# Forgetting-attention scores of a two-layer decoder trunk: float32r products over 128 stacked rows, with the forget gates' sums in a mask built on GpSimd

## The chip, the cores and the metric

The kernel runs on one core of one Trainium2 chip. The core has a matrix engine (TensorE, PE in the profile, with its weight loads shown apart as PEld), VectorE (DVE), ScalarE (ACT), GpSimd (POOL) and SyncE (SP), each working through its own instructions in order and waiting on the others through semaphores, and 16 DMA engines. The metric is device time of one execution in microseconds (us), the median over several runs; lower is better.

## The reference

Two layers of a decoder trunk over 256 tokens of width 1024: a half-step SwiGLU feed-forward, a mixer of three groups of attention heads, and another half-step feed-forward, each after an RMS norm. The change is in the third group of the mixer, C: eight heads of forgetting attention.

```python
SEQ = 256; DEPTH = 2; HEAD_DIM = 64; C_HEADS = 8; Q_BLOCK = 128

def forgetting_attention(q, k, v, log_f):
    scale = D ** -0.5
    c = jnp.cumsum(log_f, axis=1).transpose(0, 2, 1)
    def block(i):
        ...
        s = jnp.einsum('bqhd,bkhd->bhqk', qb, k).astype(jnp.float32) * scale
        s = s + cq[..., None] - c[:, :, None, :]
        s = jnp.where((key_pos[None, :] <= qpos[:, None])[None, None], s, -jnp.inf)
        p = jax.nn.softmax(s, axis=-1).astype(v.dtype)
        return jnp.einsum('bhqk,bkhd->bqhd', p, v)

cq = rms_norm(cq.reshape(B, S, C_HEADS, HEAD_DIM), c_q_norm)
ck = rms_norm(ck.reshape(B, S, C_HEADS, HEAD_DIM), c_k_norm)
log_f = jax.nn.log_sigmoid(cf.astype(jnp.float32) + forget_bias.astype(jnp.float32))
o_c = forgetting_attention(cq, ck, cv.reshape(B, S, C_HEADS, HEAD_DIM), log_f)
o_c = o_c * jax.nn.sigmoid(cg)
```

With h a head, q a query position and k a key position, a score is the scaled product plus c[q] - c[k], where c is the running sum of the log forget gates. Group A (four heads that share one key head, with a token indexer) and group B (four heads) have no such term.

## The kernel before

**Precision by splitting.** Weights arrive as float32 (tile `raw`, DMA on SyncE's queue, L91). For each unit of 128x1024, ScalarE casts the high part to float32r (`wh`, L117) and VectorE subtracts it to get the low part (`wl`, L121). This is called by `W.pump` some units ahead of their use. Products of a weight and an activation are then three float32r products instead of one in float32. Heads A and B use a cheaper form (`products`): a query of 64 columns is stacked with its own low part to 128 rows (`stack`, L718 and L719), a key is written twice to 128 rows, and the transposed key is split in a high and a low part (`keys_T`, L741 and L742). Two float32r products, high and low, then make one score. C's scores before the change are one float32 product over 66 rows: 64 of the head, one for c, one of ones. For that the tiles `cqa` and `cka` have 66 columns, the last two of which hold [c, 1] for queries and [1, -c] for keys.

**Order.** All instructions are put out in the order of the program (a manual schedule). In a mixer, the input projection runs in 32 steps (eight chunks of columns, four units each); work beside it is hung on a step number with `at_step`. `cumsum` at step 29 sums the gates by a product with a triangular matrix; `c_norm` at step 25 scales C's queries and keys on GpSimd. Then come the heads of A and C in one pipeline, together with the output projection: for i from 0 to 12, `scores(i)`, `flip(i-1)` (transposes the softmax weights), `exps(i)`, at i = 1, 3, 5, 7 `c_T` (transposes queries and keys of a pair of C heads), except at i = 3, 5, 7 and 12 a half of an output-projection block (`next(halves)`; after each second half a `W.pump`), at odd i `outT` (transposes finished outputs), and `values(i-1)`. Heads 0 to 3 are A's, 4 to 11 C's.

**Per head.** `scores` writes one PSUM bank; VectorE adds the mask, negates and takes the minimum along the row in one instruction for each query block (L1024, 128 and 256 columns); ScalarE takes the exponential (L1031, L1032); TensorE transposes (L1038); VectorE or ScalarE, by turns, copies to SBUF (L1040); TensorE multiplies with the values, which carry a column of ones for the row sum; VectorE takes the reciprocal (L1054) and scales (L1060 or L1063). PSUM tiles of the tag "gu" have four banks, the working tiles "tmp" nine buffers; both are handed round in the order in which the program asks, so that the next user waits for the last reader of the buffer's former content.

Of the kernel before, what the change touches and what calls it, by code (L numbers as in the profile page):

```python
# [10 lines left out]
F32 = mybir.dt.float32  # L11
# [130 lines left out]
def kernel(ctx: ExitStack, tc: tile.TileContext, x, ffn1_norm, ffn1_w_gate, ffn1_w_up, ffn1_w_down,  # L142
# [9 lines left out]
    sm = ctx.enter_context(tc.tile_pool(name="sm", bufs=4))  # L152
    at = ctx.enter_context(tc.tile_pool(name="at", bufs=1))
    pp = ctx.enter_context(tc.tile_pool(name="pp", bufs=2))
    psum = ctx.enter_context(tc.tile_pool(name="psum", bufs=4, space=PSUM))
    ctx.enter_context(tc.manual_schedule())

# [131 lines left out]
    cs = cst[:, 256:512].rearrange("p (t c) -> p t c", t=2)  # L289
    causal = cp.tile([P, 3 * P], F32, name="causal")  # L290
    identr = cp.tile([P, P], F32R, name="identr")
    cqa = [at.tile([P, 8, 66], F32, name=f"cqa{t}", tag=f"cqa{t}") for t in range(2)]
    cka = [at.tile([P, 8, 66], F32, name=f"cka{t}", tag=f"cka{t}") for t in range(2)]
    va = [at.tile([P, 13, 65], F32, name=f"va{t}", tag=f"va{t}") for t in range(2)]
    for t in range(2):
        G.memset(cqa[t][:, :, 65:66], 1.0)
        G.memset(cka[t][:, :, 64:65], 1.0)
        G.memset(va[t][:, :, 64:65], 1.0)


    def mm(o, l, r, start, stop):
        T.matmul(o, l, r, start=start, stop=stop, skip_group_check=True)  # L302
# [358 lines left out]
    def mixer(l, norm, nxt):  # L661
# [3 lines left out]
        def at_step(n, fn):  # L665
            side.append((n, next(count), fn))
# [7 lines left out]
        def heads(ap, n):  # L674
            return ap.rearrange("p (h d) -> p h d", h=n)
# [25 lines left out]
        def head_rs(ss, n, tag):  # L701
            return rsqrt(ss, ss, 1.0 / HD, n, tag)
# [6 lines left out]
        def evac(dst, ps, t, scale=None):  # L709
            A.activation(dst, ps, AF.Copy, scale=norm.r[:, t:t + 1])  # L710
# [33 lines left out]
        def products(o, q, k, start, stop):  # L744
            mm(o, q, k[0], start, False)
            mm(o, q, k[1], False, stop)
# [24 lines left out]
        def post_ib(ps):  # L771
# [98 lines left out]
            def cumsum():  # L870
                b = bank("acc")
                mm(b[:, 0:16], tri, lf.rearrange("p t h -> p (t h)"), True, False)
                mm(b[:, 8:16], ones, lf[:, 0], False, True)
                for t in range(2):
                    c = b[:, 8 * t:8 * t + 8]
                    A.copy(cqa[t][:, :, 64], c)
                    A.activation(cka[t][:, :, 65], c, AF.Copy, scale=-1.0)

            at_step(SUMS_STEP, cumsum)
        def post_a(ps):  # L880
            ss = sm.tile([P, 2, 5], F32, name="ssa", tag="ss")
            rot = [hp.tile([P, S], F32, name="aqr", tag="hl") for _ in range(2)]
            ak = [at.tile([P, 1, HD], F32, name=f"ak{t}", tag=f"ak{t}") for t in range(2)]
            akd = [at.tile([P, 2, HD], F32, name=f"akd{t}", tag=f"kd{t}") for t in range(2)]
            sq = []
            for t in range(2):
                evac(rot[t], ps[t][:, :256], t)
                evac(ak[t][:, 0], ps[t][:, 256:320], t)
                evac(va[t][:, 0, 0:64], ps[t][:, 320:384], t)
                sq.append(squares(ps[t][:, :320], t, 5))  # L890

            def a_rope(t):
                rope(heads(rot[t], 4), tab[:, 0, 0, t], tab[:, 0, 1, t])
                rope(ak[t], tab[:, 1, 0, t], tab[:, 1, 1, t])

            for t in range(2):
                at_step(A_ROPE + t, lambda t=t: a_rope(t))

            def a_norm():
                for t in range(2):  # L900
                    square_sums(ss[:, t], sq[t])
                rs = head_rs(ss.rearrange("p t h -> p (t h)"), 10, "a")
                for t in range(2):
                    scale_heads(akd[t], ak[t], rs[:, 5 * t + 4:5 * t + 5])
                st["ra"] = minus(rs, 10, "a")

            at_step(A_ROOT, a_norm)

            def a_split():
                st["aq"] = [stack(x) for x in rot]  # L910

            def a_turn():
                st["aqT"] = at.tile([P, 4, S], F32R, name="aqT", tag="qs")
                st["akT"] = at.tile([P, 2, 1, S], F32R, name="akT", tag="ikT")
                queries_T(st["aqT"], st["aq"])
                keys_T(st["akT"], [d.rearrange("p a b -> p (a b)")[:, None] for d in akd])

            at_step(A_TURN - 2, a_split)
            at_step(A_TURN, a_turn)
# [33 lines left out]
            run_heads([("B", h) for h in range(4)], qk_b, "acc", lambda i, fn: at_step(B_STEP + i, fn))  # L953

        c_ss = at.tile([P, 2, 2, 8], F32, name="c_ss", tag="c_ss")

        def c_sums(i, dst, ps, when):
            sq = []
            for t in range(2):
                evac(dst[t][:, :, 0:64], heads(ps[t], 8), t)  # L960
                sq.append(squares(ps[t], t, 8))

            def sums():
                for t in range(2):
                    square_sums(c_ss[:, i, t], sq[t])

            at_step(when, sums)

        def post_ck(ps):
            c_sums(0, cka, ps, 21)  # L970

        def post_cq(ps):
            c_sums(1, cqa, ps, 25)
            for t in range(2):
                q = cqa[t][:, :, 0:64]
                G.tensor_tensor(q, q, gc[:, None, :].to_broadcast([P, 8, HD]), op=ALU.mult)

            def c_norm():
                rs = head_rs(c_ss.rearrange("p i t h -> p (i t h)"), 32, "c")
                for t in range(2):  # L980
                    for i, d in enumerate((cka, cqa)):
                        x = d[t][:, :, 0:64]
                        scale_heads(x, x, rs[:, 16 * i + 8 * t:16 * i + 8 * t + 8])

            at_step(25, c_norm)

# [15 lines left out]
        def run_heads(hs, qk, tag, emit=None):  # L1002
            pj, pt, op = {}, {}, {}

            def scores(i):

                kind, h = hs[i]
                q, k = qk(kind, h)
                b = bank(tag)
                if kind == "C":  # L1010
                    mm(b[:, 0:P], q[:, 0:P], k[:, 0:P], True, True)
                    mm(b[:, P:3 * P], q[:, P:S], k[:, 0:S], False, True)
                else:
                    products(b[:, 0:P], q[:, 0:P], [c[:, 0:P] for c in k], True, True)
                    products(b[:, P:3 * P], q[:, P:S], [c[:, 0:S] for c in k], False, True)
                mask = st["amask"] if kind == "A" else causal
                s = tmp(3 * P)
                nm = sm.tile([P, 2], F32, name="nm", tag="nm")
                for t, c in enumerate((slice(0, P), slice(P, 3 * P))):
                    scale = -1.0  # L1020
                    if kind != "C":
                        col = (5 * t if kind == "A" else 4 * t) + h
                        scale = st["r" + kind.lower()][:, col:col + 1]
                    V.tensor_tensor_reduce(s[:, c], b[:, c], mask[:, c], scale, 3e38, op0=ALU.add, op1=ALU.min,  # L1024
                                           accum_out=nm[:, t:t + 1])
                pj[i] = (s, nm)
# [99 lines left out]

        halves = out_halves()

        c_both = xp.tile([P, 2, 8, S], F32, name="cT", tag="xhl")
        cT = [c_both[:, 0], c_both[:, 1]]  # L1130

        def c_T(hp_):
            for d, src in zip(cT, (cqa, cka)):
                b = bank("gu")
                for i in range(2):
                    for t in range(2):
                        T.transpose(b[:66, i * S + t * P:i * S + (t + 1) * P], src[t][:, 2 * hp_ + i, :], ident)  # L1137
                (A.copy if src is cqa else V.tensor_copy)(d[:66, 2 * hp_:2 * hp_ + 2],
                                                         b[:66].rearrange("p (a b) -> p a b", a=2))

        def qk_ac(kind, h):
            if kind == "A":
                return st["aqT"][:, h], [st["akT"][:, c, 0] for c in range(2)]
            return cT[0][:66, h], cT[1][:66, h]

        hs = [("A", h) for h in range(4)] + [("C", h) for h in range(8)]
        scores, exps, flip, values, outT = run_heads(hs, qk_ac, "gu")
        n = len(hs)
        next(halves)
        for i in range(n + 1):  # L1150
            if i < n:
                scores(i)
            if i > 0:
                flip(i - 1)
            if i < n:
                exps(i)
            if i in (1, 3, 5, 7):
                c_T(i // 2)
            if i not in (3, 5, 7, n):
                next(halves)  # L1160
            if 0 < i < n:
                if i > 2 and i % 2:
                    outT((i - 3) // 2)
                values(i - 1)
# [64 lines left out]
```

## Time and profile before

| | us |
|---|---|
| median of 3 runs | 1037.88 (1037.73 to 1037.98) |
| profiled execution | 1038.33 |
| span of its instructions | 1036.6 |
| granted TensorE clock | 1.00 |
| stage of heads A and C, layer 0 | about 291 to 327 |
| the same, layer 1 | about 804 to 843 |

The page of the profile gives for each engine its busy time and share of the span, the chain of waits that ended last, the costliest groups of instructions by line, and the DMA issues. The timeline of an engine lists start, busy time, engine, line, operation, output and inputs with partitions x elements, and in brackets the idle time before it and who ended it. Instructions of an engine overlap a little, so that the distance of two starts, and not the busy time, is what one costs; for TensorE the ends are modelled and the difference is large.

### The profile page before, as it was taken

How to read it: one execution, taken by the hardware profiler on the slowest of the kernel's cores; microseconds unless marked ns; L12 is line 12 of the kernel's file. 1: busy time of each engine (PE TensorE's matmuls, PEld its weight loads, DVE VectorE, ACT ScalarE, POOL GpSimd, SP SyncE). 2: the span in 40 equal slices, each digit the busy share in tenths (PEclk: the TensorE clock that was granted, in tenths of full speed). 3: DMA queues.
4: the chain of work that ended last, by engine and by line, in shares of the span. 5: the costliest groups of instructions: out<-in, count | busy, mean ns of one | idle time of the engine just before them, and what ended most of it. 6: DMA issues, size and time to landing. Idle time of an engine off the chain costs nothing.

```text
span 1036.6 us, 15084 instructions
## 1 busy us (share of the span) xinstructions
PE 1032.3 (100%) x5641; PEld 898.8 (87%) x5641; DVE 808.9 (78%) x1537; ACT 591.8 (57%) x1045; POOL 148.2 (14%) x177
## 2 busy tenths in 40 slices
PE   9999999999999999999999999999999999999998
PEld 8888888898888888888888888888988988888887
DVE  6978778789876877777788777787898768777776
ACT  6655555666854655555465555557676546555552
POOL 2003000167800000000000110002766000000000
PEclk9999999999999999999999999999999999999999
DMA  9674656555431364645645564664555224554631
GB/s 320 222 244 157 214 185 198 182 190 174 154 131 42 123 230 144 236 163 206 200 163 195 180 219 150 241 185 174 163 194 172 83 67 159 182 199 167 232 134 40
DMA packets 130808, 181.61 MB, mean 175 GB/s; under 512 B 7040, under 2 KB 104624, under 8 KB 130736
## 3 DMA queue, kind: packets, MB, share of 16 engines
q1 hardware_dynamic: 130704, 180.66, 51.5%
q8 instruction: 44, 0.72, 0.3%
q14 instruction: 28, 0.23, 0.1%
q10 hardware_dynamic: 32, 0.01, 0.0%
HBM read 179.60 MB, written 1.05 MB: 174 GB/s over the span
## 4 chain that ended last, share of the span: by engine, by line
PE 99%; DMA 1%; SPq 0%; DVE 0%; issue 0%
PE ps_gu L302 66%; PE ps_acc L302 30%; PE ps_acc L337 1%; PE ps_gu L1038 1%; PE ps_gu L1137 1%; DMA trunk<-in_x_dram 1%; PE ps_acc L739 0%; PE ps_acc L1038 0%; PE ps_gu L1071 0%; PE ps_acc L494 0%; SPq L91 0%; PE ps_acc L363 0%; PE ps_acc L1071 0%; SPq L190 0%; DVE trunk L376 0%
## 5 line engine op out<-in xcount | busy, mean ns | idle before, releaser
L121 DVE TENSOR_TENSOR wl<-raw,wh 128x1024 fp32r<-128x1024 f32 (+2 forms) x342 | 416.9, 1225 | 24.9 <-ACT wh L117 24.9
L117 ACT CAST wh<-raw 128x1024 fp32r<-128x1024 f32 (+2 forms) x341 | 343.0, 1036 | 5.7 <-PE ps_gu L302 4.9
L302 PE MATMUL ps_gu<-xhl,wh 128*128 128x512 f32 x1408 | 330.4, 390 | 0.0
L302 PEld LDWEIGHTS ps_gu<-xhl,wh 128*128 128x128 f32 x1408 | 262.7, 188 | 53.9 <-ACT wh L117 0.4
L302 PEld LDWEIGHTS ps_gu<-xhl,wl 128*128 128x128 f32 x1408 | 176.1, 191 | 4.2 <-issue 0.2
L302 PE MATMUL ps_gu<-xhl,wl 128*128 128x256 f32 x1408 | 179.1, 283 | 0.0
L302 PE MATMUL ps_gu<-wh,xhl 128*128 128x512 f32 (+2 forms) x512 | 157.2, 377 | 0.0
L441 DVE TENSOR_TENSOR tmp<-ps_gu,tmp 128x256 f32<-128x256 f32 x176 | 72.9, 422 | 107.7 <-ACT tmp L440 107.4
L302 PE MATMUL ps_acc<-wh,hh 128*128 128x512 f32 (+1 forms) x352 | 137.2, 390 | 0.0
L302 PE MATMUL ps_acc<-wl,hh 128*128 128x512 f32 (+1 forms) x352 | 137.0, 389 | 0.0
L302 PE MATMUL ps_acc<-wh,hl 128*128 128x512 f32 (+1 forms) x352 | 136.5, 388 | 0.0
L440 ACT COPY tmp<-ps_gu 128x256 f32<-128x256 f32 x176 | 63.5, 371 | 93.3 <-PE ps_gu L302 93.1
L302 PEld LDWEIGHTS ps_gu<-wh,xhl 128*128 128x128 f32 x512 | 94.8, 188 | 14.6
L455 ACT CAST hh<-tmp 128x256 fp32r<-128x256 f32 x80 | 32.6, 407 | 120.0 <-DVE tmp L452 120.0
L302 PE MATMUL ps_gu<-wl,xhl 128*128 128x512 f32 (+2 forms) x256 | 95.7, 374 | 0.0
L447 ACT ACTIVATE tmp<-tmp 128x256 f32<-128x256 f32 x88 | 36.9, 419 | 81.9 <-DVE tmp L445 81.6
L313 POOL TENSOR_TENSOR y_n<-msq,minus_half 128x2 f32<-128x2 f32 x6 | 6.8, 1141 | 529.7 <-DVE msq L312 529.7
L302 PEld LDWEIGHTS ps_acc<-wh,hl 128*128 128x128 f32 x352 | 66.1, 188 | 13.9
L302 PEld LDWEIGHTS ps_acc<-wh,hh 128*128 128x128 f32 x352 | 66.2, 188 | 12.6
L302 PEld LDWEIGHTS ps_acc<-wl,hh 128*128 128x128 f32 x352 | 66.3, 188 | 12.2
L302 PEld LDWEIGHTS ps_gu<-wl,xhl 128*128 128x128 f32 x256 | 48.2, 188 | 6.7
L326 ACT ACTIVATE xhl<-ps_acc,gT 128x256 fp32r<-128x256 f32 x48 | 19.1, 474 | 39.2 <-PE ps_acc L337 35.7
(221 smaller groups left out, 1010.8 us busy)
## 6 DMA issues: line engine op xcount, KB each, us to landing
raw<-in_ffn_w_down_dram SPq DMA_DIRECT2D x44, 1024.0 KB, 4.9
raw<-in_ffn_w_gate_dram SPq DMA_DIRECT2D x42, 1024.0 KB, 6.6
raw<-in_ffn_w_up_dram SPq DMA_DIRECT2D x42, 1024.0 KB, 7.5
raw<-in_w_in_dram SPq DMA_DIRECT2D x24, 1024.0 KB, 4.9
raw<-in_w_out_dram SPq DMA_DIRECT2D x8, 1024.0 KB, 4.9
raw<-in_w_in_dram SPq DMA_DIRECT2D x4, 768.0 KB, 4.9
raw<-in_w_in_dram SPq DMA_DIRECT2D x4, 656.0 KB, 4.0
raw<-in_ffn_w_gate_dram SPq DMA_DIRECT2D x3, 512.0 KB, 7.1
```

Of the source, the lines that this page charges most:

```text
L117: self.nc.scalar.copy(hv, src)
L121: (engine or self.nc.vector).tensor_tensor(lv, self.srcs[self.n_low], hv.bitcast(F32), op=ALU.subtract)
L302: T.matmul(o, l, r, start=start, stop=stop, skip_group_check=True)
L313: G.tensor_tensor(y, dst, minus_half[:, :n], op=ALU.pow)
L326: A.activation(self.h[:, m], src, AF.Copy, scale=gT[:, self.col + m:self.col + m + 1])
L337: T.transpose(ps[:, i, t * P:(t + 1) * P], trunk[:, t, (2 * mp + i) * P:(2 * mp + i + 1) * P], ident)
L440: A.copy(o, ps[:, 1])
L441: V.tensor_tensor(o, ps[:, 0], o, op=ALU.add)
L447: A.activation(th, t_, AF.Tanh, scale=0.5)
L455: (V.tensor_copy if late else A.copy)(hh, t_)
L1038: T.transpose(b[:, j * P:(j + 1) * P], pj[i][:, j * P:(j + 1) * P], ident)
L1137: T.transpose(b[:66, i * S + t * P:i * S + (t + 1) * P], src[t][:, 2 * hp_ + i, :], ident)
```

## The change

C's scores take the form that A's and B's have: two float32r products over 128 stacked rows. The term c[q] - c[k] is no longer in the product. Instead a mask of 128x384 for each head holds it together with the causal mask, and `scores` adds this mask where it added the causal one. The mask is built on GpSimd by four instructions a head (`decay`), two heads ahead. For it the sums are needed along a row, on every partition: they are transposed, negated and written to DRAM (`turn_sums`, step 30), and read back to all 128 partitions (`load_sums`, step 31, 1 MB in SBUF), both on ScalarE's DMA queue. Queries are still scaled in `c_norm`; keys are scaled on GpSimd as they are written twice, in `c_parts`, which stacks a pair's queries too. `c_T` keeps its places and writes a buffer for two pairs in turn.

```diff
@@ post_ib
                 b = bank("acc")
                 mm(b[:, 0:16], tri, lf.rearrange("p t h -> p (t h)"), True, False)
                 mm(b[:, 8:16], ones, lf[:, 0], False, True)
-                for t in range(2):
-                    c = b[:, 8 * t:8 * t + 8]
-                    A.copy(cqa[t][:, :, 64], c)
-                    A.activation(cka[t][:, :, 65], c, AF.Copy, scale=-1.0)
+                st["c"] = sm.tile([P, 2, 8], F32, name="c", tag="c", bufs=1)
+                A.copy(st["c"].rearrange("p t h -> p (t h)"), b[:, 0:16])
+
+            def turn_sums():
+                b = bank("acc")
+                for t in range(2):
+                    T.transpose(b[:8, t * P:(t + 1) * P], st["c"][:, t], ident)
+                n = tmp(S)[:8]
+                A.activation(n, b[:8, :S], AF.Copy, scale=-1.0)
+                st["row"] = dram.tile([8, S], F32, name="minus_c_row", tag="minus_c_row")
+                nc.scalar.dma_start(st["row"], n)
+
+            def load_sums():
+                d = st["row"]
+                st["minus_c"] = at.tile([P, 8, S], F32, name="minus_c", tag="kT")
+                nc.scalar.dma_start(st["minus_c"], bass.AP(tensor=d.tensor, offset=d.offset,
+                                                           ap=[[0, P], [S, 8], [1, S]]))
 
             at_step(SUMS_STEP, cumsum)
+            at_step(SUMS_STEP + 1, turn_sums)
+            at_step(SUMS_STEP + 2, load_sums)
@@ post_cq
             def c_norm():
                 rs = head_rs(c_ss.rearrange("p i t h -> p (i t h)"), 32, "c")
-                for t in range(2):
-                    for i, d in enumerate((cka, cqa)):
-                        x = d[t][:, :, 0:64]
-                        scale_heads(x, x, rs[:, 16 * i + 8 * t:16 * i + 8 * t + 8])
+                st["rk"] = rs[:, 0:16]
+                for t in range(2):
+                    scale_heads(cq[:, t], cq[:, t], rs[:, 16 + 8 * t:24 + 8 * t])
@@ scores
-                if kind == "C":
-                    mm(b[:, 0:P], q[:, 0:P], k[:, 0:P], True, True)
-                    mm(b[:, P:3 * P], q[:, P:S], k[:, 0:S], False, True)
-                else:
-                    products(b[:, 0:P], q[:, 0:P], [c[:, 0:P] for c in k], True, True)
-                    products(b[:, P:3 * P], q[:, P:S], [c[:, 0:S] for c in k], False, True)
-                mask = st["amask"] if kind == "A" else causal
+                products(b[:, 0:P], q[:, 0:P], [c[:, 0:P] for c in k], True, True)
+                products(b[:, P:3 * P], q[:, P:S], [c[:, 0:S] for c in k], False, True)
+                mask = decays.pop(h) if kind == "C" else st["amask"] if kind == "A" else causal
@@ mixer, heads A and C
-        def c_T(hp_):
-            for d, src in zip(cT, (cqa, cka)):
-                b = bank("gu")
-                for i in range(2):
-                    for t in range(2):
-                        T.transpose(b[:66, i * S + t * P:i * S + (t + 1) * P], src[t][:, 2 * hp_ + i, :], ident)
-                (A.copy if src is cqa else V.tensor_copy)(d[:66, 2 * hp_:2 * hp_ + 2],
-                                                         b[:66].rearrange("p (a b) -> p a b", a=2))
+        cT = xp.tile([P, 2, 4, 2, S], F32R, name="cT", tag="xhl")
+        beside = {}
+
+        def c_parts(j):
+            hs2 = slice(2 * j, 2 * j + 2)
+            q = tp.tile([P, 512], F32R, name="stacked", tag="tmp")
+            q4 = q.rearrange("p (t h s d) -> p t h s d", t=2, h=2, s=2)
+            A.copy(q4[:, :, :, 0], cq[:, :, hs2])
+            V.tensor_tensor(q4[:, :, :, 1], cq[:, :, hs2], q4[:, :, :, 0].bitcast(F32), op=ALU.subtract)
+            k = tmp(512)
+            k4 = k.rearrange("p (t h s d) -> p t h s d", t=2, h=2, s=2)
+            for t in range(2):
+                G.tensor_tensor(k4[:, t], ck[:, t, hs2, None, :].to_broadcast([P, 2, 2, HD]),
+                                st["rk"][:, 8 * t + 2 * j:8 * t + 2 * j + 2, None, None].to_broadcast([P, 2, 2, HD]),
+                                op=ALU.mult)
+            beside[j] = [x.rearrange("p (t h c) -> p t h c", t=2, h=2) for x in (q, k)]
+
+        def c_T(j):
+            q, k = beside.pop(j)
+            d = cT[:, j % 2]
+            bq, bk = bank("gu"), bank("gu")
+            for i in range(2):
+                for t in range(2):
+                    mm(bq[:, i * S + t * P:i * S + (t + 1) * P], q[:, t, i], identr, i + t == 0, True)
+            for i in range(2):
+                for t in range(2):
+                    T.transpose(bk[:, i * S + t * P:i * S + (t + 1) * P], k[:, t, i], ident)
+            bq, bk = (b.rearrange("p (h s) -> p h s", h=2) for b in (bq, bk))
+            A.copy(d[:, 0], bq)
+            A.copy(d[:, 1], bk)
+            V.tensor_tensor(d[:, 2], bk, d[:, 1].bitcast(F32), op=ALU.subtract)
+
+        def decay(h):
+            m = tmp(3 * P)
+            for t, (c, n) in enumerate(((slice(0, P), P), (slice(P, 3 * P), S))):
+                G.tensor_scalar(m[:, c], st["minus_c"][:, h, :n], st["c"][:, t, h:h + 1], None, op0=ALU.add)
+            for c in (slice(0, P), slice(2 * P, 3 * P)):
+                G.tensor_tensor(m[:, c], m[:, c], causal[:, c], op=ALU.add)
+            decays[h] = m
@@ the pipeline
+        c_parts(0)
         next(halves)
         for i in range(n + 1):
             ...
             if i in (1, 3, 5, 7):
                 c_T(i // 2)
+            if i in (2, 4, 6):
+                c_parts(i // 2)
+            if 2 <= i < 10:
+                decay(i - 2)
             if i not in (3, 5, 7, n):
                 next(halves)
```

More of the change, by code (lines that the diff above doesn't have):

```diff
@@ L154 @@
     pp = ctx.enter_context(tc.tile_pool(name="pp", bufs=2))
+    dram = ctx.enter_context(tc.tile_pool(name="dram", bufs=1, space=bass.MemoryType.DRAM))
     psum = ctx.enter_context(tc.tile_pool(name="psum", bufs=4, space=PSUM))
@@ L291 @@
     identr = cp.tile([P, P], F32R, name="identr")
-    cqa = [at.tile([P, 8, 66], F32, name=f"cqa{t}", tag=f"cqa{t}") for t in range(2)]
-    cka = [at.tile([P, 8, 66], F32, name=f"cka{t}", tag=f"cka{t}") for t in range(2)]
+    cq = at.tile([P, 2, 8, HD], F32, name="cq", tag="cq")
+    ck = at.tile([P, 2, 8, HD], F32, name="ck", tag="ck")
     va = [at.tile([P, 13, 65], F32, name=f"va{t}", tag=f"va{t}") for t in range(2)]
     for t in range(2):
-        G.memset(cqa[t][:, :, 65:66], 1.0)
-        G.memset(cka[t][:, :, 64:65], 1.0)
         G.memset(va[t][:, :, 64:65], 1.0)
@@ L955, in mixer @@
         c_ss = at.tile([P, 2, 2, 8], F32, name="c_ss", tag="c_ss")
+        decays = {}
         def c_sums(i, dst, ps, when):
@@ L959, in c_sums @@
             for t in range(2):
-                evac(dst[t][:, :, 0:64], heads(ps[t], 8), t)
+                evac(dst[:, t], heads(ps[t], 8), t)
                 sq.append(squares(ps[t], t, 8))
@@ L969, in post_ck @@
         def post_ck(ps):
-            c_sums(0, cka, ps, 21)
+            c_sums(0, ck, ps, 21)
         def post_cq(ps):
-            c_sums(1, cqa, ps, 25)
+            c_sums(1, cq, ps, 25)
             for t in range(2):
-                q = cqa[t][:, :, 0:64]
+                q = cq[:, t]
                 G.tensor_tensor(q, q, gc[:, None, :].to_broadcast([P, 8, HD]), op=ALU.mult)
@@ L1127, in mixer @@
         halves = out_halves()
-        c_both = xp.tile([P, 2, 8, S], F32, name="cT", tag="xhl")
-        cT = [c_both[:, 0], c_both[:, 1]]
-        def c_T(hp_):
-            for d, src in zip(cT, (cqa, cka)):
-                b = bank("gu")
-                for i in range(2):
-                    for t in range(2):
-                        T.transpose(b[:66, i * S + t * P:i * S + (t + 1) * P], src[t][:, 2 * hp_ + i, :], ident)
-                (A.copy if src is cqa else V.tensor_copy)(d[:66, 2 * hp_:2 * hp_ + 2],
-                                                         b[:66].rearrange("p (a b) -> p a b", a=2))
+        cT = xp.tile([P, 2, 4, 2, S], F32R, name="cT", tag="xhl")
@@ L1143, in qk_ac @@
                 return st["aqT"][:, h], [st["akT"][:, c, 0] for c in range(2)]
-            return cT[0][:66, h], cT[1][:66, h]
+            d = cT[:, h // 2 % 2]
+            return d[:, 0, h % 2], [d[:, 1, h % 2], d[:, 2, h % 2]]
         hs = [("A", h) for h in range(4)] + [("C", h) for h in range(8)]
```

## The prediction

> **What bounds the kernel now.** I read the page first, then the matmul engine's timeline through the stretch in which heads A and C are scored, then VectorE's and ScalarE's in the same stretch. Part 1 of the page and the chain of waits say that TensorE is the bound almost everywhere:
>
> ```profile
> PE 1032.3 (100%) x5641; PEld 898.8 (87%) x5641; DVE 808.9 (78%) x1537; ACT 591.8 (57%) x1045; POOL 148.2 (14%) x177
> ...
> PE 99%; DMA 1%; SPq 0%; DVE 0%; issue 0%
> ```
>
> So a cheaper product is worth its whole saving, but only as long as TensorE stays without gaps; and any wait that TensorE gains is a loss in full. The stage that changes runs from 291 to 327 us in layer 0 (and 804 to 843 in layer 1), in iterations i = 0 to 12: scores of head i, transposes ("flip") of head i-1, then in some iterations the transposes of a C pair (c_T) or half a block of the output projection, then the values of head i-1. TensorE's timeline (start, busy, engine, line, operation):
>
> ```profile
> 293.21 0.49 PE L1038 MATMUL ps_gu<-ident,p 128*128 128x128 f32 x3
> ...
> 296.93 0.49 PE L1038 MATMUL ps_gu<-ident,p 128*128 128x128 f32 x3
> ...
> 299.23 0.71 PE L302 MATMUL ps_gu<-akT,aqT 128*128 128x128 f32 x4
> 299.78 0.49 PE L1038 MATMUL ps_gu<-ident,p 128*128 128x128 f32 x3
> 300.11 0.60 PE L1137 MATMUL ps_gu<-ident,cqa 128*66 128x128 f32 x4
> 300.54 0.60 PE L1137 MATMUL ps_gu<-ident,cka 128*66 128x128 f32 x4
> 300.98 0.38 PE L1071 MATMUL ps_gu<-ident,o 128*128 128x128 f32 x2
> 301.27 0.88 PE L302 MATMUL ps_gu<-va,pT 128*128 128x65 f32 x6
> 301.99 0.87 PE L302 MATMUL ps_gu<-cT 66*128 66x128 f32 x4
> 302.70 0.49 PE L1038 MATMUL ps_gu<-ident,p 128*128 128x128 f32 x3
> ...
> 305.04 0.87 PE L302 MATMUL ps_gu<-cT 66*128 66x128 f32 x4
> ...
> 308.55 0.49 PE L1038 MATMUL ps_gu<-ident,p 128*128 128x128 f32 x3
> ...
> 314.40 0.49 PE L1038 MATMUL ps_gu<-ident,p 128*128 128x128 f32 x3
> ```
>
> The starts give the true prices, since busy times overlap. The flips of heads 1, 3, 5 and 7 (296.93, 302.70, 308.55, 314.40) are 5.77, 5.85 and 5.85 us apart, 17.47 together. These are my yardstick. VectorE and ScalarE over the first of these periods:
>
> ```profile
> 291.65 0.34 DVE L1024 CUSTOM_DVE_ANT_0 tmp<-ps_gu,amask,minus_a 128x128 f32<-128x128 f32 x1
> ...
> 297.81 1.22 DVE L121 TENSOR_TENSOR wl<-raw,wh 128x1024 fp32r<-128x1024 f32 x1
> 299.46 0.17 DVE L1054 RECIPROCAL ri<-ps_gu 128x2 f32<-128x2 f32 x1 [0.43 <-PE ps_gu L302]
> ...
> 299.98 0.35 DVE L1024 CUSTOM_DVE_ANT_0 tmp<-ps_gu,amask,minus_a 128x128 f32<-128x128 f32 x1
> ...
> 300.66 0.56 DVE L1040 COPY pT<-ps_gu 128x384 f32<-128x384 f32 x1
> 301.18 0.69 DVE L1138 COPY cT<-ps_gu 66x512 f32<-66x512 f32 x1
> ```
>
> ```profile
> 292.45 0.51 ACT L1032 ACTIVATE p<-tmp,nm 128x256 f32<-128x256 f32 x1
> ...
> 298.13 0.50 ACT L1032 ACTIVATE p<-tmp,nm 128x256 f32<-128x256 f32 x1
> ...
> 300.78 0.51 ACT L1032 ACTIVATE p<-tmp,nm 128x256 f32<-128x256 f32 x1
> ```
>
> The reader should see how little room there is in the iterations without a half of the output projection (3, 5, 7). VectorE's copy of the flipped weights ends at 301.22 and the values that read it start at 301.27. VectorE's whole slack in the first period is the 0.43 us before the reciprocal. An engine that is "78% busy" is here the second bound.
>
> **The change part by part: TensorE.** A C head's two fp32 products show as four records and cost 0.71 us (301.99 to 302.70); four float32r products of the same widths cost head A 0.55 (299.23 to 299.78). The saving is 0.16 us a head, 2.6 us for 16 heads. Transposing queries through the float32r identity costs (1.09-0.27)/7 = 0.117 each by the row below, against (0.60-0.27)/3 = 0.11 for today's, 0.27 being one record; four per pair make +0.03, eight pairs +0.24. The key transposes keep their number and streamed width: nothing. The sums' turn adds two transposes; such a pair costs 0.29 (outputs, 300.98 to 301.27), so 0.3 a layer, 0.6 in all. If nothing else moved, the sum were -2.6 + 0.24 + 0.6, about -1.8 us.
>
> ```profile
> 271.09 1.09 PE L302 MATMUL ps_acc<-identr,stacked 128*128 128x128 f32 x8
> ...
> 280.88 0.29 PE L302 MATMUL ps_acc<-lf,cst 128*128 128x16 f32 x2
> ```
>
> **The new chain in c_T.** Now one ScalarE copy and one VectorE copy run side by side, one for each PSUM bank. After the change ScalarE casts both banks in turn, and VectorE's subtraction of the keys waits for the second cast. The same pair of operations exists for B's keys, and the stacking for A's and B's queries (min/median/max in ns):
>
> ```profile
> L741 ACT CAST bkT<-ps_acc x4: 607/616/624, 243.2 to 756.8; 128x512 fp32r<-128x512 f32 x4
> L742 DVE TENSOR_TENSOR bkT<-ps_acc,bkT x4: 673/674/676, 246.9 to 760.6; 128x512 fp32r<-128x512 f32 x4
> ```
>
> ```profile
> L719 DVE TENSOR_TENSOR stacked<-bqr,stacked x4: 956/959/964, 233.9 to 747.8; 128x256 fp32r<-128x256 f32 x4
> L718 ACT CAST stacked<-aqr x4: 401/406/412, 262.6 to 776.0; 128x256 fp32r<-128x256 f32 x4
> L719 DVE TENSOR_TENSOR stacked<-aqr,stacked x4: 414/414/414, 263.6 to 777.0; 128x256 fp32r<-128x256 f32 x4
> ```
>
> The tag of these PSUM tiles has four banks, handed round in order. In iteration 5 they go to scores 5, flip 4, the two of c_T, outputs, values 4, scores 6, flip 5: so flip 5 takes the bank that the key subtraction still reads. Queued on VectorE behind that subtraction are the low parts of the outputs, the reciprocal, the output scaling and the next reduce.
>
> **The new chain in c_parts.** In iterations 2, 4 and 6 a 0.41 us copy stands on ScalarE behind the exponentials of head i, and VectorE's 0.41 us subtraction waits for it, with the weights' wl subtraction, the reciprocal and the next head's reduce queued behind.
>
> Worked for the first period, with the rows' durations and ScalarE's instructions overlapping by about 0.09 as they do now. Exponentials 2 end at 298.63; copy to 298.95; subtraction to 299.41, where VectorE before had worked on wl since 297.81; wl to 300.55; reciprocal, and 0.52 after its start the reduce of head 3 at 300.97 instead of 299.98. The flipped weights are copied at 302.20 (300.66 + 0.56, plus 0.99), values 2 start at 302.25 instead of 301.27. Exponentials 3 end 1.31 after the reduce begins (300.78 + 0.51 against 299.98), at 302.28; query cast to 302.8, key cast to 303.3; subtraction to 304.02; flip 3 at 304.07 instead of 302.70. **+1.37.**
>
> Second period (no wl, so the wait for the copy is covered by VectorE's idle time): flip 3 to scores 5 is still 2.34 us (302.70 to 305.04), scores 5 at 306.4, its reduce 0.13 late at 307.26, exponentials to 308.5, casts to 309.55, subtraction to 310.27, flip 5 at 310.32. That is 6.25 instead of 5.85. **+0.40**, with 0.16 saved on each of two scores and overrun by the casts.
>
> Third period (wl again): exponentials 6 end at 312.35, copy 312.67, subtraction 313.13, wl 314.27, reciprocal and scaling, reduce 7 at 314.80; flipped weights 315.90; exponentials 7 to 316.0, casts to 317.05, subtraction 317.77, flip 7 at 317.82: 7.50 instead of 5.85. **+1.65.** What is late next is every later instruction of TensorE, nothing absorbs it; from then on VectorE catches up, and heads 9 to 11 save 3 x 0.16 = 0.48.
>
> At the start the first subtraction of c_parts stands ahead of head 0's reduce (291.65): 0.41 later, against a slack of 0.25 between exponentials 0 (to 292.96) and flip 0 (293.21): +0.2. A layer: 1.37 + 0.40 + 1.65 - 0.48 + 0.2 + 0.3 = 3.4; two layers **+6.9 us**. Bounds: -1.8 in all if every cast and copy were covered, and upward the locks that follow.
>
> **GpSimd beside VectorE.** GpSimd is empty in this stage today. It gets, per head, 128 and 256 columns of tensor_scalar and twice 128 of tensor_tensor, and per pair twice 256 columns for the keys. Rows:
>
> ```profile
> 204.38 0.46 POOL L684 TENSOR_TENSOR swapped<-iqr,cst 128x128 f32<-128x128 f32 x1
> ...
> 217.52 0.75 POOL L686 TENSOR_TENSOR bqr<-bqr,swapped 128x256 f32<-128x256 f32 x1
> ...
> 277.19 1.05 POOL L691 TENSOR_TENSOR cqa<-cqa,y_c 128x512 f32<-128x512 f32 x1
> 278.19 2.03 POOL L691 TENSOR_TENSOR cka<-cka,y_c 128x512 f32<-128x512 f32 x1
> ```
>
> ```profile
> 277.25 4.05 DVE L121 TENSOR_TENSOR wl<-raw,wh 128x1024 fp32r<-128x1024 f32 x2
> ```
>
> No row has a tensor_scalar of that size with a column operand; I price it as the two-input rows (between nothing and twice that). A mask is 3 x 0.46 + 0.75 = 2.13 us, eight of them 17, the keys 8 x 0.75 = 6: 23 us a layer. The last rows show the two engines taking turns: two wl take 4.05 us beside GpSimd instead of 2 x 1.22, and GpSimd's 1.05 becomes 2.03; the stacking subtraction above takes 0.96 beside GpSimd and 0.41 without. So the subtraction may cost +0.5 and wl between +0.4 and +0.8, twice a layer on the path (periods one and three): between 0 and 2.6 a layer. I take 1.25, a half, since GpSimd waits for buffers part of the time: **+2.5 us.**
>
> [...]
>
> **The round trip through DRAM.** The sums' turn comes one step after the sums (280.88), the load one step later. An 8 KB transfer on ScalarE's queue landed in 2.6 us, 1 MB in 1 KB pieces in 6.6:
>
> ```profile
> raw<-in_ffn_w_gate_dram SPq DMA_DIRECT2D x42, 1024.0 KB, 6.6
> ...
> tmp<-in_ffn_norm_dram ACTq DMA_DIRECT2D x1, 8.0 KB, 2.6
> ```
>
> With steps of about 3 us the read is issued at 287 to 288 and lands at about 295; mask 0 is done by 297.5 and is read at 302. Cost nothing; the cover is 4 to 5 us. While ScalarE waits for the write, weight casts are queued behind, seven units ahead of their use. The small copies that go (four of the sums, GpSimd's two key scalings) lie beside other work.
>
> **Sum.** The profiled execution took 1038.33 us (span 1036.6), 0.45 over the median. 6.9 + 2.5 = 9.4: 1047.7 for such an execution, **1047.3 us** against the median.
>
> **Rivals.** (1) *The saving arrives.* If ScalarE and VectorE ran ahead enough, TensorE alone decides: 1037.88 - 1.8 = 1036.1, or 1035.3 without the turn's and cast's extras. For it: TensorE is the bound in 99% of the chain. Against: 0.05 us between copy and values. (2) *Half hidden.* The casts cost but c_parts' copy finds a gap: periods at +0.4 each, 1.2 - 0.48 + 0.5 = 1.2 a layer: 1040.3. (3) *GpSimd becomes the bound.* If its rows in company (2.03 for 1.05) hold for most of its instructions, 23 us become 37; begun at 295 they end at 332, where head 11 wants its mask near 323: +9 a layer, 1056. The same if the broadcast lands 9 us late. The point from which it decides is some 28 us of GpSimd work a layer. [...]
>
> **Chances.** Forecast 0.6, rival 1 0.12, rival 2 0.13, rival 3 0.15. The range takes in the forecast with its unknowns (6.9 less 4 to 6.9 plus 5.2, and somewhat over) and rival 2: 1039.5 to 1053. What a measurement of this kernel can tell from no change is 0.2%, 2.1 us; of rival 1 half lies beyond it. Faster 0.07, same 0.10, slower 0.83.
>
> **What would show it.** Right: flips of heads 3, 5 and 7 about 7, 6.3 and 7.5 to 8 us apart from the ones before, TensorE's idle time there put down to VectorE's key subtraction and to the flipped weights' copy, C scores at 0.55. Wrong: flips still under 5.85 apart (rival 1); the reduces of C waiting for GpSimd (rival 3); C scores not cheaper than 0.71, or VectorE reaching reduce 3 within 0.2 us of the scores' end.

## The result, and the profile after

| | before | after |
|---|---|---|
| median of 6 runs each, us | 1037.93 (1037.73 to 1038.24) | 1044.36 (1044.07 to 1044.82) |
| ratio | | 1.0062, 95% interval 1.0049 to 1.0075 |
| profiled execution, us (span) | 1038.33 (1036.6) | 1044.18 (1042.5) |

The change costs 6.4 us; 9.4 were forecast, and the time lies in the stated range. Parts 1 and 4 of the page after:

```profile
PE 1032.5 (99%) x5645; PEld 897.6 (86%) x5645; DVE 810.0 (78%) x1545; ACT 599.3 (57%) x1057; POOL 197.4 (19%) x249
...
PE 96%; ACT 2%; DVE 2%; issue 0%; POOL 0%; ACTq 0%; POOLq 0%
```

VectorE, at 0% before, and ScalarE, not among the entries before, now hold 4% of the chain. GpSimd's 49 us more hold none of it. TensorE's timeline in layer 0 (in brackets idle time and its releaser):

```profile
293.13 0.49 PE L1050 MATMUL ps_gu<-ident,p 128*128 128x128 f32 x3
...
296.83 0.49 PE L1050 MATMUL ps_gu<-ident,p 128*128 128x128 f32 x3
...
299.93 0.64 PE L301 MATMUL ps_gu<-identr,stacked 128*128 128x128 f32 x4
301.29 0.63 PE L1168 MATMUL ps_gu<-ident,tmp 128*128 128x128 f32 x4 [0.72 <-DVE o L1075]
301.87 0.44 PE L1083 MATMUL ps_gu<-ident,o 128*128 128x128 f32 x2
302.34 0.88 PE L301 MATMUL ps_gu<-va,pT 128*128 128x65 f32 x6
...
304.09 0.55 PE L1050 MATMUL ps_gu<-ident,p 128*128 128x128 f32 x3 [0.36 <-DVE cT L1172]
...
306.46 0.71 PE L301 MATMUL ps_gu<-cT 128*128 128x128 f32 x4
307.00 0.49 PE L1050 MATMUL ps_gu<-ident,p 128*128 128x128 f32 x3
...
310.24 0.55 PE L1050 MATMUL ps_gu<-ident,p 128*128 128x128 f32 x3 [0.36 <-DVE cT L1172]
...
314.88 0.63 PE L1168 MATMUL ps_gu<-ident,tmp 128*128 128x128 f32 x4 [0.84 <-DVE o L1072]
...
317.56 0.55 PE L1050 MATMUL ps_gu<-ident,p 128*128 128x128 f32 x3 [0.37 <-DVE cT L1172]
```

Flips 1, 3, 5 and 7 stand at 296.83, 304.09, 310.24 and 317.56: the periods are 7.26, 6.15 and 7.32 us, against 5.77, 5.85 and 5.85. That is +3.26 for the three. Heads 8 to 11 take back some: the flip of head 11 comes 2.66 us later than before in layer 0 (328.94 for 326.28), and layer 1 adds 2.74 between the flips of heads 0 and 11. Together 5.4 us of the span's 5.9. A quarter of a microsecond more is the turn of the sums in layer 1: from the gates' product to head 0's scores TensorE takes 10.26 us there, 10.01 before. The rest falls behind TensorE's last product. A product's cheapness is there: 0.54 us from the scores of head 5 (306.46) to the next flip, where 0.71 stood.

VectorE and ScalarE over the first period:

```profile
298.87 0.74 DVE L1150 TENSOR_TENSOR stacked<-cq,stacked 128x256 fp32r<-128x256 f32 x1 [1.07 <-ACT stacked L1149]
299.53 1.21 DVE L121 TENSOR_TENSOR wl<-raw,wh 128x1024 fp32r<-128x1024 f32 x1
...
300.85 0.29 DVE L1075 TENSOR_TENSOR o<-ps_gu,ri 128x128 f32<-128x128 f32 x1
301.06 0.34 DVE L1036 CUSTOM_DVE_ANT_0 tmp<-ps_gu,amask,minus_a 128x128 f32<-128x128 f32 x1
...
303.35 0.69 DVE L1172 TENSOR_TENSOR cT<-ps_gu,cT 128x512 fp32r<-128x512 f32 x1 [1.06 <-ACT cT L1171]
```

```profile
298.44 0.39 ACT L1149 CAST stacked<-cq 128x256 fp32r<-128x256 f32 x1
...
302.26 0.56 ACT L1170 CAST cT<-ps_gu 128x512 fp32r<-128x512 f32 x1
302.73 0.59 ACT L1171 CAST cT<-ps_gu 128x512 fp32r<-128x512 f32 x1
```

Read from top to bottom: VectorE stands idle 1.07 us until ScalarE's stacking copy, which had its own exponentials ahead of it. The weight subtraction starts at 299.53 instead of 297.81. So the scaling of an output and the reduce of head 3 come a microsecond late, and TensorE waits for that scaling, because the key transposes take the PSUM bank that it frees. Later VectorE is idle again, 1.06 us, for the second cast, and flip 3 waits for the subtraction behind it. GpSimd in the same stretch:

```profile
292.71 2.28 POOL L1178 TENSOR_SCALAR tmp<-minus_c,c 128x128 f32<-128x128 f32 x2 [10.37 <-DMA minus_c<-minus_c_row]
...
299.30 2.73 POOL L1178 TENSOR_SCALAR tmp<-minus_c,c 128x128 f32<-128x128 f32 x2
302.00 0.87 POOL L1180 TENSOR_TENSOR tmp<-tmp,causal 128x128 f32<-128x128 f32 x2
302.85 1.50 POOL L1178 TENSOR_SCALAR tmp<-minus_c,c 128x128 f32<-128x128 f32 x2
```

The sums land at 292.7, and no mask is late. While VectorE's weight subtraction runs undisturbed (1.21 us), the pair of instructions on GpSimd takes 2.73 us instead of 1.50: it is GpSimd that waits.

### The profile page after: what moved, and what is told of

Its sections match the earlier page's. It is cut to its first block, busy times and chain, and to the rows that moved or that the text cites. A ratio compares the mean times of both kernels' runs of the same rounds, so it can differ in the third digit from the quotient of the medians.

```text
span 1042.5 us, 15212 instructions
## 1 busy us (share of the span) xinstructions
PE 1032.5 (99%) x5645; PEld 897.6 (86%) x5645; DVE 810.0 (78%) x1545; ACT 599.3 (57%) x1057; POOL 197.4 (19%) x249
## 3 DMA queue, kind: packets, MB, share of 16 engines
HBM read 181.70 MB, written 1.06 MB: 175 GB/s over the span
## 4 chain that ended last, share of the span: by engine, by line
PE 96%; ACT 2%; DVE 2%; issue 0%; POOL 0%; ACTq 0%; POOLq 0%
PE ps_gu L301 65%; PE ps_acc L301 29%; PE ps_acc L336 1%; PE ps_gu L1050 1%; ACT p L1044 0%; ACT p L1043 0%; DVE wl L121 0%; DVE cT L1172 0%; DVE stacked L1150 0%; ACT cT L1171 0%; ACT cT L1170 0%; PE ps_acc L738 0%; PE ps_acc L1050 0%; PE ps_acc L493 0%; ACT stacked L1149 0%
```

## The experiments

Theory: TensorE waits for two chains between ScalarE and VectorE, that of the stacking (c_parts) and that of the casts (c_T). Main rival: GpSimd's masks cost the time, by slowing VectorE's instructions beside them or by being late. Where the expectations say "port" for the first of these, the runs show the longer times alone: in the changed kernel the stacking subtraction took 0.42 to 0.74 us and GpSimd's pair up to 2.73 for 1.50, and no run set apart what makes them longer. Each run is compared with the kernel before on the same chip; the ratios have 95% intervals. The kernel before had a median of 1037.82 us beside runs 1 to 4, 1038.09 beside 5 to 7, 1038.08 beside 8 and 9 and 1038.11 beside 10, so differences of two medians from different chips carry up to 0.3 us of the chips. The edits are against the changed kernel.

**1. Stacking ahead of the flip.** ScalarE is idle while it waits for a flip; the copy is put there.

```diff
                 scores(i)
+            if i in (2, 4, 6):
+                c_parts(i // 2)
             if i > 0:
                 flip(i - 1)
@@
-            if i in (2, 4, 6):
-                c_parts(i // 2)
```

> The changed kernel, with the stacking of C's queries (c_parts at i = 2, 4, 6) put out right after the scores of head i, ahead of its flip and exponentials, so that ScalarE's copy falls into its idle time. Theory (VectorE's queue waits behind that copy): the flips of heads 3 and 7 come 6.1 to 6.3 us after the flips of heads 1 and 5, where they came 7.26 and 7.32 after; some 2.1 us a layer, 1040 us in all. Rival (GpSimd's masks cost the time, through VectorE's port or by being late): GpSimd's work is unchanged, so 1043.5 to 1044.5 us and the periods stay over 7.

Measured 1040.63 us, ratio 1.0028 (1.0018 to 1.0039). TensorE's timeline, the three later flips:

```profile
302.99 0.55 PE L1050 MATMUL ps_gu<-ident,p 128*128 128x128 f32 x3 [0.36 <-DVE cT L1172]
...
309.14 0.55 PE L1050 MATMUL ps_gu<-ident,p 128*128 128x128 f32 x3 [0.37 <-DVE cT L1172]
...
315.72 0.55 PE L1050 MATMUL ps_gu<-ident,p 128*128 128x128 f32 x3 [0.37 <-DVE cT L1172]
```

With flip 1 at 296.89 the periods are 6.10, 6.15 and 6.58. The waits for the output scaling are gone, those for the key subtraction are all there. 3.7 us come back from the place of one copy, with GpSimd's work unchanged: more than half of the loss is the stacking's chain. The third period is 0.3 longer than expected.

**2. No masks.** `decay` is not called and C's heads add the causal mask alone, so the forget gates' sums are left out of the scores. GpSimd keeps the scaling of the keys.

```diff
-            if 2 <= i < 10:
-                decay(i - 2)
@@
-                mask = decays.pop(h) if kind == "C" else st["amask"] if kind == "A" else causal
+                mask = st["amask"] if kind == "A" else causal
```

> The changed kernel without decay: C's heads add the causal mask alone, so the forget gates' sums are left out of the scores; the sums are still turned and loaded. Theory: the stalls stay, only the stacking subtraction loses its 0.1 to 0.3 us beside GpSimd: 1043.3 to 1044.2 us. Rival (GpSimd beside VectorE was priced at 2.5 us in the forecast): 1042 us or below.

Measured 1043.44 us, ratio 1.0054 (1.0041 to 1.0066), 0.9 us below the changed kernel's median. The stalls remain (0.41 and 0.80 us for the output scaling, 0.36 three times for the key subtraction). Against the kernel before on each chip the difference is 0.8 us, and between flips 0 and 11 it is 0.34 and 0.31 us in the two layers. The rival is out as the main cause; 0.9 is about the most that the masks can have cost here.

**3. The query cast on VectorE.**

```diff
-            A.copy(d[:, 0], bq)
+            V.tensor_copy(d[:, 0], bq)
             A.copy(d[:, 1], bk)
```

> The changed kernel with the cast of C's transposed queries on VectorE instead of ScalarE, so that the two banks of c_T are emptied side by side as before the change. Theory (flip i waits for the bank which the key subtraction reads, at the end of a chain exponentials, cast, cast, subtraction): the three periods 0.4 to 0.5 us shorter each, 2.4 to 3 us in all: 1041.4 to 1042 us. Rival (VectorE is the bound of the stage, whatever it does there delays): 0.69 us more for VectorE per pair, not faster than 1044 us.

Measured 1042.74 us, ratio 1.0043 (1.0031 to 1.0056): 1.6 us gained, where 2.4 to 3 were expected. The five executions are of two kinds: 1041.51 and 1041.59 us at a granted clock of 1.000, and 1042.74 to 1043.31 us at 0.998. At the full clock the gain is 2.8 us, inside the expectation; the median lies among the others. The profiled execution is of the first kind (1041.59), so no trace shows where the clock fell. In its TensorE timeline no flip waits for the key subtraction any more, but the other wait has grown:

```profile
300.95 0.63 PE L1168 MATMUL ps_gu<-ident,tmp 128*128 128x128 f32 x4 [0.71 <-DVE o L1075]
...
313.91 0.63 PE L1168 MATMUL ps_gu<-ident,tmp 128*128 128x128 f32 x4 [1.18 <-DVE o L1072]
```

The periods are 6.76, 5.67 and 7.17: 0.50, 0.48 and 0.15 shorter. In the last one the wait is 1.18 us instead of 0.84: VectorE has 0.68 us more to do per pair, and where its queue is already late, part of the gain is lost.

**4. Both.** 

> Both edits: stacking ahead of the flip, query cast on VectorE. Theory: the two waits are separate and add up: periods 5.7 to 5.9, TensorE nearly without gaps, 1036 to 1037.5 us, which is no slower than the kernel before. Rival (the gains overlap, or another wait takes their place): 1038.5 to 1041 us.

Measured 1037.66 us, ratio 0.9999 (0.9990 to 1.0008): no slower than before, and a little above the band. Together the two edits give back 6.7 us. That is about the sum of run 1's 3.7 and the 2.8 of run 3 at the full clock, so the waits are separate. The periods are 5.69, 5.66 and 6.02 in layer 0 and 6.03, 5.66 and 6.03 in layer 1; the last one is still longer than before the change.

**5. The last pair stacked at i = 4,** away from the weight subtraction at i = 6.

```diff
-            if i in (2, 4, 6):
+            if i in (2, 4):
                 c_parts(i // 2)
+            if i == 4:
+                c_parts(3)
```

> Both edits of the run before, and the stacking of the last pair moved from i = 6 (where a weight subtraction stands on VectorE too) to i = 4 (where none does). Theory: the period from flip 5 to flip 7, 6.02 us there, falls to 5.65 to 5.75; 0.6 us for two layers: 1036.8 to 1037.3 us. Rival (the key transposes of that iteration wait for something else): the period stays near 6.0 and the time at 1037.5 or above.

Measured 1037.63 us, ratio 0.9998 (0.9989 to 1.0006). The period in question fell as expected, to 5.74 (308.25 to 313.99), in layer 1 too. But the first one of layer 0 rose from 5.69 to 6.04, and the median stayed; set against the kernel before on each chip, run 5 is 0.3 us better than run 4, which is within the noise. VectorE's timeline in that first period, which the edit did not touch:

```profile
297.42 0.73 DVE L1150 TENSOR_TENSOR stacked<-cq,stacked 128x256 fp32r<-128x256 f32 x1
298.08 1.63 DVE L121 TENSOR_TENSOR wl<-raw,wh 128x1024 fp32r<-128x1024 f32 x1
```

In layer 0 of run 4 the same two took 0.53 and 1.48, in its layer 1 already 0.73 and 1.63, with a first period of 6.03; without masks (run 7) they take 0.42 and 1.22, and the period is 5.61 in both layers. So this is GpSimd's price on VectorE, and within one program it differs from layer to layer: a stacking and a weight subtraction in one iteration can pay it twice. Whether it depends on which instruction of GpSimd is under way, no run shows.

**6. GpSimd's headroom.** Run 5 with the masks' first additions done twice (the masks stay the same).

```diff
-                G.tensor_scalar(m[:, c], st["minus_c"][:, h, :n], ...)
+                for _ in range(2):
+                    G.tensor_scalar(m[:, c], st["minus_c"][:, h, :n], ...)
```

> As the run above, with each mask's first additions (tensor_scalar, 128 and 256 columns) done twice over, so that GpSimd has about 12 us more a layer, 36 instead of 24; the masks are the same. Theory (GpSimd has slack until its work from the landing of the sums fills the time to head 11's reduce, some 29 us): the last mask is done at 293.5 + 8 x 3.9 + 2.4 = 327 us or later, where head 11 wants it at 323; the reduces of the later heads wait for it, 4 to 6 us a layer: 1045 to 1049 us. Rival (GpSimd's work costs little whatever its length): below 1040 us.

Measured 1053.34 us, ratio 1.0142 (1.0126 to 1.0158), above the band. A reduce that waits for its mask, GpSimd's last mask of layer 0, and the work of all engines with the granted clock in two stretches (columns: stretch, its length, then busy time of PE, PEld, DVE, ACT, POOL, clock, DMA share, GB/s):

```profile
313.98 0.29 DVE L1036 CUSTOM_DVE_ANT_0 tmp<-ps_gu,tmp 128x128 f32<-128x128 f32 x1 [2.25 <-POOL tmp L1181]
...
327.16 3.22 POOL L1179 TENSOR_SCALAR tmp<-minus_c,c 128x128 f32<-128x128 f32 x4
330.35 0.87 POOL L1181 TENSOR_TENSOR tmp<-tmp,causal 128x128 f32<-128x128 f32 x2
```

```profile
312.00:316.00 4.00, 1.71 (x14) 1.24 (x13) 1.91 (x7) 1.54 (x4) 3.81 (x7) 1.00 0.00 0
...
324.00:328.00 4.00, 4.00 (x17) 3.48 (x17) 2.25 (x9) 1.83 (x5) 3.81 (x6) 0.57 0.00 0
```

The reduces of the later heads wait for GpSimd, as expected, by up to 2.25 us. The last mask is done at 331.2, where 327 or later was expected, and after TensorE's second gap the granted clock is 0.57 in the mean over 4 us, which no expectation had. The masks do decide once their work fills the stage: 24 us a layer has room, 36 has not.

**7. Runs 4 and 2 together.** 

> The two edits (stacking ahead, query cast on VectorE) without decay: the forget gates' sums are left out of the scores. Theory (GpSimd's port costs VectorE a few tenths in the stacking and once in a weight subtraction, 1.48 for 1.22 us): 1036.9 to 1037.5 us, the period from flip 5 to flip 7 about 0.2 shorter. Rival (the saving of TensorE is eaten by GpSimd): 1036.2 us or below.

Measured 1037.02 us, ratio 0.9989 (0.9980 to 0.9998); 0.6 us below run 4 in the medians, 0.9 when each is set against the kernel before on its chip. Between flips 0 and 11 it is 0.25 and 0.63 us shorter in the two layers, and the period from flip 5 to flip 7 is 5.83, 0.2 shorter, as expected. The stacking subtraction in the two, the first row of run 4 and the second of this one:

```profile
L1150 DVE TENSOR_TENSOR stacked<-cq,stacked x8: 418/572/730, 291.2 to 822.3; 128x256 fp32r<-128x256 f32 x8
```

```profile
L1150 DVE TENSOR_TENSOR stacked<-cq,stacked x8: 418/420/422, 292.1 to 822.6; 128x256 fp32r<-128x256 f32 x8
```

Without masks the spread is gone. GpSimd's share of the loss is some tenths of a microsecond a layer.

**8 and 9. Stacking in the input projection.** Both have the query cast on VectorE and pairs 0 and 1 stacked at steps 31 and 32. Run 8 stacks pairs 2 and 3 at i = 4. Run 9 stacks them at i = 2 and 6, and moves the weight subtractions to the other halves.

```diff
+        at_step(31, lambda: c_parts(0))
+        at_step(32, lambda: c_parts(1))
@@ run 8
+            if i == 4:
+                c_parts(2)
+                c_parts(3)
@@ run 9
+            if i in (2, 6):
+                c_parts(i // 4 + 2)
@@ run 9, out_halves
-                    if hf == 1:
+                    if hf == 0:
                         W.pump()
```

> Query cast on VectorE; the stacking of pairs 0 and 1 as steps 31 and 32 of the input projection, where no flip waits for VectorE, that of pairs 2 and 3 at i = 4 after the scores. Theory: no stacking and no weight subtraction stand in the same iteration, so all three periods are 5.6 to 5.75 us (17.0 for the three, 17.47 before the change) and the cheaper scores of heads 9 to 11 come on top: 1036.0 to 1037.0 us. Rival (weight subtractions beside GpSimd's masks cost by themselves): one of the periods stays above 5.9, 1037.3 us or more.

> Query cast on VectorE; pairs 0 and 1 stacked in the projection, pairs 2 and 3 at i = 2 and 6; the weight subtractions moved by one half of the output projection, from i = 0, 2, 6, 9, 11 to the half before i = 0 and i = 1, 4, 8, 10, so that i = 2 and 6 have none. Theory: as the run beside it, 1036.0 to 1037.0 us. Rival (the weight subtraction at i = 1 falls on the chain of c_T there): the period from flip 1 to flip 3 starts late, 1037.3 us or more.

Both missed: 1040.07 us, ratio 1.0018 (1.0009 to 1.0026), and 1045.49 us, ratio 1.0065 (1.0053 to 1.0077). Not at the place I watched: in run 8 the periods are 5.61, 5.67 and 5.66, as expected. The loss is at head 0. First run 8 (VectorE's first stacking, then TensorE's flip 0), then run 9 with its clock:

```profile
286.59 0.42 DVE L1109 TENSOR_TENSOR stacked<-cq,stacked 128x256 fp32r<-128x256 f32 x1 [1.39 <-ACT stacked L1108]
```

```profile
294.39 0.33 PE L1050 MATMUL ps_gu<-ident,p 128*128 128x128 f32 x1 [1.06 <-ACT p L1043]
```

```profile
296.11 0.33 PE L1050 MATMUL ps_gu<-ident,p 128*128 128x128 f32 x1 [2.20 <-ACT p L1043]
```

```profile
293.00:297.00 4.00, 1.61 (x11) 1.15 (x10) 3.34 (x11) 3.03 (x7) 0.33 (x1) 1.00 0.83 264
297.00:301.00 4.00, 4.00 (x20) 3.47 (x19) 3.04 (x4) 2.10 (x4) 4.00 (x6) 0.63 0.00 0
```

At the end of the projection VectorE's queue (selection of keys, A's mask, the gate, the first reduce) is the path to head 0, and the stacking stood in it: VectorE waited 1.39 us for ScalarE's copy, which is queued behind ScalarE's part in the turn of the sums. It is the fault of the changed kernel again, at another place. In run 9 a weight subtraction stood there too. The clock then makes run 9 worse: its executions take 1043.3 us at a granted clock of 0.998 and 1046.6 at 0.995.

**10. Pair 1 at i = 1 instead,** pair 0 as in the change, pairs 2 and 3 at i = 4, query cast on VectorE.

```diff
                 scores(i)
+            if i == 1:
+                c_parts(1)
+            if i == 4:
+                c_parts(2)
+                c_parts(3)
```

> Query cast on VectorE; pair 0 stacked where the change has it, pair 1 at i = 1 right after the scores, pairs 2 and 3 at i = 4. Theory: VectorE has 0.5 us free at i = 1, so head 0's flip stays where it is, and the three periods are the 5.61, 5.67 and 5.66 us of the run with two pairs stacked in the projection: 1036.5 to 1037.3 us, faster than before by 0.05 to 0.15%. Rival (the stacking at i = 1 pushes the key subtraction of the first pair onto flip 1): 1037.5 us or more.

Measured 1036.83 us, ratio 0.9988 (0.9979 to 0.9997), faster than both kernels. TensorE's flips 1, 3, 5 and 7:

```profile
296.66 0.49 PE L1050 MATMUL ps_gu<-ident,p 128*128 128x128 f32 x3
...
302.27 0.55 PE L1050 MATMUL ps_gu<-ident,p 128*128 128x128 f32 x3
...
307.94 0.55 PE L1050 MATMUL ps_gu<-ident,p 128*128 128x128 f32 x3
...
313.60 0.55 PE L1050 MATMUL ps_gu<-ident,p 128*128 128x128 f32 x3
```

The periods are 5.61, 5.67 and 5.66, and the timeline shows no gap of TensorE in this stage. The float32r products bring a gain at last, some 1.3 us against the 1.8 that TensorE's terms alone had come to; the interval reaches from 0.3 to 2.2 us. The traces say the same: between flips 0 and 11 run 10 is 1.05 and 1.04 us shorter than before, and the turn of the sums takes back a quarter of a microsecond a layer.

## Why the prediction was right, and which terms were off

- *TensorE's own terms.* Right: 0.54 us for a C head's scores instead of 0.71, and (0.64-0.27)/3 = 0.12 for a transpose through the identity. The turn of the sums, priced at 0.3 us a layer, costs 0.26 and 0.25: from the gates' product to head 0's scores TensorE takes 10.27 us (layer 0, the two rows below), and 10.01 before (280.88 to 290.89).

```profile
280.58 0.29 PE L301 MATMUL ps_acc<-lf,cst 128*128 128x16 f32 x2
...
290.85 0.62 PE L301 MATMUL ps_gu<-akT,aqT 128*128 128x128 f32 x4
```

- *The chain in c_T.* Right in place and size: the middle period, in which the stacking costs nothing (run 1 left it at 6.15), is 6.15 for 6.25; ScalarE's second cast ends it, and run 3 removed the wait by emptying the two banks side by side.
- *The chain in c_parts.* Shown by run 1, and right in size to a quarter of a microsecond. That 7.26 and 7.32 lie so near the forecast's 7.14 and 7.50 is in part luck: the forecast's figures leave GpSimd out. Without masks (run 2) the periods are 6.95, 6.15 and 7.28, so the chains alone were priced 0.5 us a layer too high. The place where TensorE first stops was put wrong: not the values waiting for the flipped weights, but already the key transposes, which wait for the bank that VectorE's output scaling frees.
- *The start.* The 0.2 us at flip 0 did not come: 293.13 for 293.21.
- *GpSimd beside VectorE.* The step that was mis-sized: 2.5 us in the sum, 0.8 by run 2 and 0.9 by run 7, each against the kernel before on its chip. The forecast let VectorE lose half of all encounters; in the changed kernel the weight subtraction kept its 1.21 us and GpSimd waited. The trace before had a sign of this that the forecast misread. It took A's stacking subtraction (0.41 us at 263.6) for one without GpSimd, but GpSimd had the pair below under way, whose instructions took 3.14 and 0.39 us; the first of them had waited.

```profile
262.63 3.50 POOL L691 TENSOR_TENSOR akd<-ak,y_a 128x128 f32<-128x128 f32 x2
```

GpSimd (1.6 us too much), the chains (1.0) and the start (0.4) together make up the 3 us between forecast and result.

- *Of the rivals,* the one in which the saving arrives describes run 10, not the changed kernel. The half-hidden one (1040.3 us) comes close to run 1 (1040.63), where the stacking's copy was given its gap. That of late masks was right about its point: 24 us of GpSimd's work fit, 36 did not. The broadcast landed in 6.9 us, priced at 6.6.

The forecast charged GpSimd's company to the weight subtraction and the stacking subtraction alone. The rows of the changed kernel fit that for the key subtraction, which has one input in PSUM: with the masks running it kept 0.69 us (0.690 to 0.692 in all eight), while the stacking subtraction, with both inputs in SBUF, went from 0.42 to as much as 0.74. That the place of the inputs decides was not shown.

## What to carry to other kernels

Where one engine is busy without gaps, price a change there and then follow the engines that feed it in the order of their queues: here 1.8 us of cheaper products cost 6.4, mostly since a 0.4 us copy stood behind the wrong instruction and two PSUM banks were emptied one after the other. An instruction that waits for another engine belongs where its own engine is idle and the producer has already passed; before moving it, look what is queued behind it there, because the stacking moved into the projection lost some 2 us (run 8) and more (run 9) against run 4. Check the first head, or tile, of a pipeline by itself.

## What was not expected of the hardware

- *The clock.* After a gap of 2.20 us TensorE's granted clock fell to 0.50 in run 9: in stretches of 1 us from 298 to 302 it is 0.53, 0.50, 0.50 and 0.76, 1.7 us of full clock lost. The weight products of the output projection start 0.43 us apart there (298.35 to 300.06), 0.23 ahead of the gap. In run 6 the first gap of layer 0, 2.26 us, left the clock at 1.00; it fell at about 324 us, after a second gap of 1.79 us (0.57 in the mean from 324 to 328). In layer 1 the same gap was followed by the fall:

```profile
314.88 0.44 PE L1083 MATMUL ps_gu<-ident,o 128*128 128x128 f32 x2 [2.26 <-DVE nm L1036]
...
834.59 0.44 PE L1083 MATMUL ps_gu<-ident,o 128*128 128x128 f32 x2 [2.26 <-DVE nm L1036]
```

```profile
836.00:840.00 4.00, 4.00 (x17) 3.35 (x16) 1.89 (x9) 1.39 (x3) 3.81 (x7) 0.57 0.01 2
```

So the length of the gap alone does not decide; what does is open. The 0.84 us of the changed kernel left the clock at 1.00 in all its executions; with run 3's longest gap of 1.18 us three of five executions show 0.998.
- *GpSimd's tensor_scalar.* With one input and a column operand the undisturbed pair of 128 and 256 columns takes 1.50 us, the shortest of them 0.60, so about 0.6 and 0.9; a tensor_tensor with two inputs took 0.46 and 0.61 at these widths (medians of 32 and 16).
